# Moving filler work between two attention stages: memory gates earlier, forget sums later, two pairs of branch products begun early

## The chip, the cores and the metric

One core of a Trainium2 chip runs the whole program; the other cores are idle. The metric is device microseconds from the first to the last instruction of one execution, as a median over runs of the same program, lower is better.

## The reference

A decoder trunk of two layers on 512 tokens of width 1024. Each layer is a half-weighted SwiGLU block, a mixing block and a second half-weighted SwiGLU block, each between two RMS norms. The change lies in the mixing block, which is, cut to what matters:

```python
u = _rmsnorm(h, mix_pre_g[l])
q_sb, k_sb, v_sb, q_fx, k_fx, v_fx, f_logit, q_mem = jnp.split(u @ w_in[l], split_at, axis=-1)
o_sb = _stick_breaking_attention(q_sb, k_sb, v_sb)            # 8 heads of width 64
log_f = jax.nn.log_sigmoid(f_logit + b_forget[l])
o_fx = _forgetting_attention(q_fx, k_fx, v_fx, log_f)         # 8 heads of width 64
o_mem = _memory_attention(q_mem, k_mem, v_mem)                # 4 heads of width 128
g_sb, g_fx, g_mem = jnp.split(jax.nn.sigmoid(u @ w_gate[l] + b_gate[l]), 3, axis=-1)
merged = g_sb * (o_sb @ w_br_sb[l]) + g_fx * (o_fx @ w_br_fox[l]) + g_mem * (o_mem @ w_br_mem[l])
h = h + _rmsnorm(merged @ w_out[l], mix_post_g[l])
```

The stick-breaking weights come from a reversed running sum over the keys. The forgetting scores get a difference of running sums of `log_f`, ahead of a causal softmax. Both are row-wise work on 512 x 512 score tiles.

## The kernel before, in words

**Precision.** Every weight and activation is split into a rounded part and a remainder: ScalarE writes the rounded part (line 190 or 193), VectorE the remainder (line 191 or 194). A product is three matmuls into one PSUM bank (lines 216 to 218). Heavy products are 512 columns wide.

**Two streams on one TensorE.** In the mixing stage two streams of work are woven together by the program itself, before anything runs:

- The *chains* are the attention heads. A causal head has three steps on TensorE: the scores (`zs`, line 1305, for stick-breaking; `zf`, lines 1349 to 1357, for forgetting), ten 128 x 128 transposes of the probabilities (`pts` or `ptf`, line 1291, in `transposed`), and the product with the values (`pvs` or `pvf`, line 1278, in `attend`). Between the first two lies a row-wise chain on ScalarE and VectorE: for stick-breaking Abs, Exp, Ln (lines 1310 to 1312), an add (1313), a scan (1318), a subtraction (1321) and Exp (1322); for forgetting a maximum (1359), Exp (1361), a reciprocal (1362) and a scaling (1363). Heads come in pairs, first the four stick-breaking pairs, then the four forgetting pairs in the order 2, 3, 0, 1.
- The *queue* (`Q`) is a list of jobs that need no head at that moment: projections of the next pair (`pq`, `pk`), of values (`pv`), products of a finished branch with its output matrix (`pb`), memory gates (`pg`). A job is cut into single products; `weave` hands them out one at a time while a chain waits for its row-wise work. Each wait of a chain has a planned length in microseconds of TensorE work (12.0 and 4.7 for stick-breaking, 6.0 and 4.2 for forgetting), and a pair of heads has a *limit*, a place in the list that the queue may not pass while that pair runs. The limits of the stick-breaking pairs are cut at `marks["sb"]`, which stands just ahead of the first stick-breaking branch product, since that product needs all stick-breaking heads.

Where the list has no job left below the limit, the chain's next step follows directly, and TensorE stands still until the row-wise chain is done. The Tile framework then orders each engine's instructions by the order of the program and its own look at dependences, and each engine runs its list in that order.

**Jobs that the change moves.**

- `mem_gate(dp)` makes one pair of memory gates: 48 matmuls for two 128 x 512 tiles, two weight tiles to split, then Exp (204), a minimum (205), Ln (206), an add with maximum (211), Exp (212) and the product with the sum so far, `mg` (1651). There are four pairs; pairs 0 and 1 stand beside the first two stick-breaking pairs, pairs 2 and 3 beside the last two forgetting pairs.
- `forget_cumsum` makes the running sums `cs` of the forget logits: four transposes into `pfl` (1438), Abs, Exp, Ln on ScalarE, an add and a scan on VectorE (1445, 1446), and copies with their remainder to four places (1449 to 1452). Each forgetting head reads `cs` through `qk` (1340). It stands between the query and the key projection of the first forgetting pair.
- `merge(br, w, dp)` multiplies a branch by its output matrix (two tiles `pb`, each of four k-steps of three matmuls), fetches the saved gates `ga` from HBM by a DMA that GpSimd issues (1674), and adds gate times product to `mg` (1681, 1682). For the forgetting branch (`br` = 1) the four k-steps come in the order of the pairs 2, 3, 0, 1, so that the first three can be done before the last pair is finished. `early` = 3 cuts them off as a job of their own, `begin`, whose products (9 matmuls for each of two tiles) may be done while the last head runs; `run` does the fourth k-step and the rest. Before the change only the first of four pairs of tiles has this.

**Buffers.** PSUM has two rings of four banks: `mm` for products and `z` for scores and transposes. Row-wise tiles of the heads, the gates `ga` and the sums of `attend` share one ring of five SBUF tiles (`f32t`). Split weights have four buffers each, raw weights four.

Of the kernel before, what the change touches and what calls it, by code (L numbers as in the profile page):

```python
# [22 lines left out]
def kernel(  # L23
# [39 lines left out]
    _, S, D = x.shape  # L63
# [3 lines left out]
    ND = D // P  # L67
# [32 lines left out]
    def tmp(name):  # L100
        return sb.tile([P, S], F32, tag="f32t", bufs=5, name=name)
# [6 lines left out]
    def blk(tag, name):  # L108
        return stile([P, 2, S], tag, name)

    def pbank(tag, name):
        return ps.tile([P, S], F32, tag=tag, bufs=4, name=name)
# [95 lines left out]
    def sigmoid_neg(t, z, bias):  # L208

        log1p_exp(t, z, bias=bias)  # L210
        nc.vector.scalar_tensor_tensor(t, z, bias, t, ALU.add, ALU.max)
        nc.scalar.activation(t, t, AF.Exp, scale=-1.0)
# [7 lines left out]
    def gemm(pt, units, m, act, order=None, part=slice(None)):  # L220

        tiles = [(un, k) for un in units for k in range(un.nk)]
        order = order or range(len(tiles))
        for n in range(len(tiles))[part]:
            un, k = tiles[order[n]]
            c = slice(m * P, (m + 1) * P)
            ah, al = act(un.k0 + k)
            mm3(pt, un.h[:, k, c], un.l[:, k, c], ah, al, n == 0, n == len(tiles) - 1)
            yield 3 * pt.shape[1] * PE_US
# [5 lines left out]
    def list_act(ts):  # L235
        return lambda k, c=FULL: (ts[k][:, 0, c], ts[k][:, 1, c])
# [183 lines left out]
    def wpair(src, ktiles, c0, name, scale=None):  # L420

        return [Unit(src, k, min(4, ktiles - k), c0, 256, f"{name}_{k}", scale) for k in range(0, ktiles, 4)]
# [110 lines left out]
    Q = Queue()  # L533
# [895 lines left out]
    FOX = (2, 3, 0, 1)  # L1429

    def forget_cumsum(l, fl, holder):

        pt = pbank("mm", f"pfl{l}")
        for t in range(NT):
            nc.tensor.transpose(pt[:NH, t * P:(t + 1) * P], fl[:, t], ident[:])
        yield 0.3
        a, b = tmp(f"fa{l}")[:NH], tmp(f"fb{l}")[:NH]  # L1440

        nc.scalar.activation(a, pt[:NH], AF.Abs, bias=bfor[:, l:l + 1])
        nc.scalar.activation(a, a, AF.Exp, scale=-1.0)
        nc.scalar.activation(a, a, AF.Ln, bias=one_t[:NH])
        nc.vector.scalar_tensor_tensor(a, pt[:NH], nbfor[:, l:l + 1], a, ALU.min, ALU.subtract)
        nc.vector.tensor_tensor_scan(b, bfor[:, l:l + 1].broadcast_to([NH, S]), a, 0.0, ALU.add, ALU.add)
        cs = stile([P, S], "cs", f"cs{l}")
        nc.gpsimd.memset(cs[:].bitcast(F32), 0.0)
        nc.scalar.copy(cs[0:NH], b)
        nc.vector.tensor_tensor(cs[32:32 + NH], b, cs[0:NH].bitcast(F32), ALU.subtract)  # L1450
        for c in (0, 32):
            nc.gpsimd.tensor_copy(cs[64 + c:64 + c + NH], cs[c:c + NH])
        holder["cs"] = cs

    def mixing(l, src, ks, vs, values, dst):
# [5 lines left out]
        st, marks = {}, {}  # L1461
# [56 lines left out]
        def proj(key, un, scale):  # L1518
            nm = f"{key[0]}{l}_{key[1]}_{key[2]}"
            pt = pbank("mm", "p" + nm)  # L1520
            yield from gemm(pt[:], [un], 0, act)
            if key[0] == "q":

                t = st[key] = blk("q", nm)
                for r, ro, j in HEAD_ROWS:
                    split(t[r, j], t[ro, j], pt[r], scale=scale)
            else:

                twice = key[1] == 0
                t = st[key] = stile([P, 4 if twice else 3, S], "k", nm)  # L1530
                for r, ro, j in HEAD_ROWS:
                    split(t[r, j], t[r, 2 + j if twice else 2], pt[r])
                    if twice:
                        nc.gpsimd.tensor_copy(t[ro, j::2], t[r, j::2])
                    else:
                        nc.gpsimd.tensor_copy(t[ro, j], t[r, j])
# [15 lines left out]
        def project(br, p):  # L1552
            base = br * 1536
            marks["before", br, p] = len(Q.jobs)
            for x, off, scale in (("q", 0, 0.125), ("k", 512, None)):
                un1 = Unit(w_in[l], 0, ND, base + off + p * P, P, f"{x}{l}_{br}_{p}")
                marks[br, p] = Q.add([un1], lambda x=x, un1=un1, scale=scale: proj((x, br, p), un1, scale))
                if (br, p, x) == (1, FOX[0], "q"):
                    Q.add([], lambda: forget_cumsum(l, st["fl"], st))

        def factor(n):
# [78 lines left out]
        def mem_gate(dp):  # L1640
            ug = wpair(w_gate[l], ND, 2 * D + dp * 256, f"wg{l}_2_{dp}", scale=-1.0)

            def run():
                for m in range(2):
                    d = 2 * dp + m
                    pg = pbank("mm", f"pg{l}_2_{d}")
                    yield from gemm(pg[:], ug, m, act)
                    a = tmp(f"ga{l}_2_{d}")
                    sigmoid_neg(a[:], pg[:], nbgate[:, l, 2 * ND + d:2 * ND + d + 1])
                    md = st["merged"][dp][:, m]  # L1650
                    nc.vector.tensor_tensor(md, md, a[:], ALU.mult)
            Q.add(ug, run)

        def merge(br, w_br, dp, early=0):

            ub = wpair(w_br[l], NP, dp * 256, f"wb{l}_{br}_{dp}", scale=0.5)
            order = FOX if br == 1 else None
            gate, banks = [], []

            def products(m, part):  # L1660
                if len(banks) <= m:
                    banks.append(pbank("mm", f"pb{l}_{br}_{2 * dp + m}"))
                yield from gemm(banks[m][:], ub, m, list_act(st["o", br]), order, part)

            def begin():
                for m in range(2):
                    yield from products(m, slice(0, early))

            def run():
                for m in range(2):  # L1670
                    d = 2 * dp + m
                    gate.append(tmp(f"ga{l}_{br}_{d}"))
                    c = slice(d % 4 * S // 2, (d % 4 + 1) * S // 2)
                    nc.gpsimd.dma_start(gate[m][:].rearrange("p (i q) -> p i q", i=2),
                                        gsave[br, :, d // 4, :, c].rearrange("i p q -> p i q"))
                for m in range(2):
                    d = 2 * dp + m
                    a = gate[m]
                    yield from products(m, slice(early, NP))
                    md = st["merged"][d // 2][:, d % 2]  # L1680
                    nc.vector.scalar_tensor_tensor(a[:], a[:], 1.0, banks[m][:], ALU.add, ALU.mult)
                    nc.vector.tensor_tensor(md, md, a[:], ALU.add)
                    if br == 1:
                        mt = blk("v" if d < 4 else "qk"[d % 2], f"ms{l}_{d}")
                        split(mt[:, 0], mt[:, 1], md)
                        st["ms"].append(mt)

            if early:
                marks["begun", br] = Q.add(ub, begin)
                return Q.add([], run)  # L1690
            return Q.add(ub, run)

        marks["values"] = values
# [40 lines left out]

        heads = [(0, p) for p in range(NP)] + [(1, p) for p in FOX]
        project(*heads[0])
        project_v(*heads[0])
        marks["v"] = len(Q.jobs)
        for i, (br, _) in enumerate(heads):
            if i + 1 < len(heads):  # L1740
                project(*heads[i + 1])
            if br == 0:
                mem_branch(i)
                if i < 2:
                    mem_gate(i)
            else:
                if 4 < i < 7:
                    mem_gate(i - 3)
                if i == NP:
                    marks["sb"] = len(Q.jobs)  # L1750
                merge(0, w_br_sb, i - NP)
            if i in (2, 4):
                project_v(*heads[i + 2])
        marks["fox"] = len(Q.jobs)
        for dp in range(ND // 2):
            merge(1, w_br_fox, dp, 3 if dp == 0 else 0)


        limits = [marks["before", *h] for h in heads[2:]] + [marks["fox"], marks["begun", 1]]
# [183 lines left out]
    for l in LAYERS:  # L1943
        i, mn = 3 * l, []
# [42 lines left out]
```

## Time and profile before

| | |
|---|---|
| median of 3 runs | 2380.63 us (2379.75 to 2381.37) |
| the profiled execution, timed | 2379.89 us |
| span of the profiled execution | 2378.0 us |
| mean granted TensorE clock | 0.995 |
| causal heads, layer 0 | about 510 to 792 us of the span |
| causal heads, layer 1 | about 1689 to 1971 us of the span |

The two layers run the same program, so a stall in one is looked for in the other 1179 us later. In the profile PE is TensorE, DVE is VectorE, ACT is ScalarE, POOL is GpSimd. Rows of the timeline give the start, the duration, the engine, the line, the tiles written and read without buffer numbers, and in brackets the idle time of that engine just before with the instruction that ended it. A matmul's own duration (0.39 us at 512 columns) is longer than the distance between two of them, since they overlap; where work is counted, the distance of the starts is used.

### The profile page before, as it was taken

Reading aid. Unit: us, or ns where it says so; the run is one execution under the profiler, and the core shown is the slowest. Engines: PE = TensorE matmul, PEld = TensorE weight load, DVE = VectorE, ACT = ScalarE, POOL = GpSimd, SP = SyncE. Lnnn points to the kernel's source line nnn. Section 1 sums busy time; section 2 is a strip of 40 time slices with the busy share of each in tenths; the row PEclk is TensorE's granted clock in tenths of the full one; section 3 lists DMA queues with packets and bytes.
Section 4 is the critical chain, followed back from the end, with each engine's and each line's share of the span. In section 5 each row is a group of like instructions: output and inputs, shape, how many; then the busy total and the mean of one; then the engine's idle time right before and its main releaser. Section 6 shows DMA issues by size and latency. Waiting matters only on the chain.

```text
span 2378.0 us, 32025 instructions
## 1 busy us (share of the span) xinstructions
PE 2341.7 (98%) x11944; PEld 1991.1 (84%) x11944; DVE 1828.2 (77%) x2443; ACT 1484.0 (62%) x2406; POOL 255.3 (11%) x290
## 2 busy tenths in 40 slices
PE   9999999999989999999999999999998999999998
PEld 8888889988878788888888888899887888888887
DVE  8766978758877887769787679777688777866696
ACT  6656765667755465566665566657677554655574
POOL 1101001001112101101011110010011121110110
PEclk9999999999999999999999999999999999999999
DMA  8866858532312676759486767584322226876682
GB/s 248 235 173 182 226 190 234 167 109 63 89 54 80 219 217 168 193 151 263 161 220 170 188 191 224 188 242 138 107 72 81 63 89 213 222 186 177 181 226 98
DMA packets 237407, 398.03 MB, mean 167 GB/s; under 512 B 12458, under 2 KB 86466, under 8 KB 236740
## 3 DMA queue, kind: packets, MB, share of 16 engines
q1 hardware_dynamic: 197472, 312.06, 40.2%
q0 software_dynamic: 37472, 75.54, 17.3%
q10 hardware_dynamic: 2308, 8.39, 0.9%
q8 instruction: 94, 1.54, 0.3%
q14 instruction: 61, 0.50, 0.1%
HBM read 372.87 MB, written 23.07 MB: 167 GB/s over the span
## 4 chain that ended last, share of the span: by engine, by line
PE 88%; DVE 6%; issue 3%; DMA 2%; ACT 2%; DVEq 0%; SPq 0%; POOLq 0%; ACTq 0%
PE ptc L216 5%; PE ptc L218 5%; PE ptc L217 5%; PE pta L216 5%; PE pta L218 5%; PE pta L217 5%; PE pda L217 3%; PE pda L216 3%; PE pda L218 3%; PE pdc L218 3%; PE pdc L217 3%; PE pdc L216 3%; PE g L216 2%; PE g L218 2%; PE g L217 2%
## 5 line engine op out<-in xcount | busy, mean ns | idle before, releaser
L191 DVE TENSOR_TENSOR wl_tc<-ktc,wh_tc 128x1024 fp32r<-128x1024 f32 x80 | 97.7, 1223 | 63.3 <-ACT wh_tc L190 63.3
L191 DVE TENSOR_TENSOR wl_ta<-kta,wh_ta 128x1024 fp32r<-128x1024 f32 x80 | 97.6, 1223 | 57.7 <-ACT wh_ta L190 57.7
L190 ACT CAST wh_tc<-ktc 128x1024 fp32r<-128x1024 f32 x80 | 84.1, 1053 | 67.9 <-PE ptc L218 48.0
L218 PE MATMUL pta<-wh_ta,aga 128*128 128x512 f32 x320 | 124.7, 390 | 1.2 <-DVE aga L191 1.2
L216 PE MATMUL pta<-wh_ta,aga 128*128 128x512 f32 x320 | 125.4, 392 | 0.4 <-DVE sa L715 0.4
L216 PE MATMUL ptc<-wh_tc,agc 128*128 128x512 f32 x320 | 125.2, 393 | 0.0
L190 ACT CAST wh_ta<-kta 128x1024 fp32r<-128x1024 f32 x80 | 84.2, 1053 | 64.9 <-PE pta L218 41.8
L218 PE MATMUL ptc<-wh_tc,agc 128*128 128x512 f32 x320 | 124.6, 389 | 0.0
L217 PE MATMUL ptc<-wl_tc,agc 128*128 128x512 f32 x320 | 124.6, 389 | 0.0
L217 PE MATMUL pta<-wl_ta,aga 128*128 128x512 f32 x320 | 124.6, 389 | 0.0
L191 DVE TENSOR_TENSOR wl_ta<-raw_ta,wh_ta 128x1024 fp32r<-128x1024 f32 x58 | 70.9, 1223 | 44.6 <-ACT wh_ta L190 44.4
L191 DVE TENSOR_TENSOR wl_tc<-raw_tc,wh_tc 128x1024 fp32r<-128x1024 f32 x56 | 68.5, 1224 | 45.6 <-ACT wh_tc L190 45.6
L190 ACT CAST wh_ta<-raw_ta 128x1024 fp32r<-128x1024 f32 x58 | 60.9, 1052 | 48.3 <-PE pta L218 38.0
L190 ACT CAST wh_tc<-raw_tc 128x1024 fp32r<-128x1024 f32 x56 | 59.0, 1053 | 48.3 <-PE ptc L218 36.9
L216 PE MATMUL ptc<-wh_tc,us_b 128*128 128x512 f32 x224 | 87.7, 391 | 0.2
L216 PE MATMUL pda<-wh_da,aa 128*128 128x512 f32 x224 | 87.5, 391 | 0.0
L216 PE MATMUL pdc<-wh_dc,ac 128*128 128x512 f32 x224 | 87.5, 391 | 0.0
L218 PE MATMUL ptc<-wh_tc,us_b 128*128 128x512 f32 x224 | 87.2, 389 | 0.0
L218 PE MATMUL pda<-wh_da,aa 128*128 128x512 f32 x224 | 87.2, 389 | 0.0
L217 PE MATMUL ptc<-wl_tc,us_b 128*128 128x512 f32 x224 | 87.2, 389 | 0.0
L217 PE MATMUL pda<-wl_da,aa 128*128 128x512 f32 x224 | 87.2, 389 | 0.0
L217 PE MATMUL pdc<-wl_dc,ac 128*128 128x512 f32 x224 | 87.2, 389 | 0.0
(613 smaller groups left out, 7937.4 us busy)
## 6 DMA issues: line engine op xcount, KB each, us to landing
raw_ta<-in_ffn_w_gate_dram SPq DMA_DIRECT2D x44, 512.0 KB, 4.2
raw_wg<-in_w_gate_dram SPq DMA_DIRECT2D x44, 512.0 KB, 3.8
raw_tc<-in_ffn_w_gate_dram SPq DMA_DIRECT2D x44, 512.0 KB, 4.2
raw_da<-in_ffn_w_down_dram SPq DMA_DIRECT2D x42, 512.0 KB, 3.7
raw_dc<-in_ffn_w_down_dram SPq DMA_DIRECT2D x42, 512.0 KB, 3.3
kta<-in_ffn_w_up_dram SPq DMA_DIRECT2D x40, 512.0 KB, 6.1
ktc<-in_ffn_w_up_dram SPq DMA_DIRECT2D x40, 512.0 KB, 6.0
raw_wo<-in_w_out_dram SPq DMA_DIRECT2D x24, 512.0 KB, 3.4
```

The source lines that it names most:

```text
L190: both = [nc.scalar.copy(h_ap, src)]
L191: make = lambda: nc.vector.tensor_tensor(l_ap, src, h_ap.bitcast(F32), ALU.subtract)
L216: nc.tensor.matmul(pt, lh, rh, start=start, stop=False, skip_group_check=free)
L217: nc.tensor.matmul(pt, lh, rl, start=False, stop=False, skip_group_check=free)
L218: nc.tensor.matmul(pt, ll, rh, start=False, stop=stop, skip_group_check=free)
```

## The change

Three edits in the list of jobs, each for both layers.

- The memory gates of pairs 2 and 3 no longer stand beside the forgetting pairs 0 and 1. They stand behind the memory branch's last product at the fourth stick-breaking pair, ahead of the place `marks["sb"]`, and so below the limit of the last stick-breaking pair.
- `forget_cumsum` stands behind the key projection of the first forgetting pair, not ahead of it.
- The forgetting branch's second pair of products gets `early` = 3 too, and its two tiles are taken from the `z` ring. Both `begin` jobs are put ahead of both `run` jobs, and the limit of the last head stays at the first `begin`.

No instruction's work changes; what changes is the order on each engine, and with it which buffers follow each other in the rings.

```diff
-                if (br, p, x) == (1, FOX[0], "q"):
+                if (br, p, x) == (1, FOX[0], "k"):
                     Q.add([], lambda: forget_cumsum(l, st["fl"], st))
...
-        def merge(br, w_br, dp, early=0):
+        def merge(br, w_br, dp, early=0, tag="mm"):
...
-                    banks.append(pbank("mm", f"pb{l}_{br}_{2 * dp + m}"))
+                    banks.append(pbank(tag, f"pb{l}_{br}_{2 * dp + m}"))
...
             if early:
-                marks["begun", br] = Q.add(ub, begin)
-                return Q.add([], run)
+                marks["begun", br] = min(marks.get(("begun", br), 1 << 20), Q.add(ub, begin))
+                return lambda: Q.add([], run)
             return Q.add(ub, run)
...
             if br == 0:
                 mem_branch(i)
-                if i < 2:
-                    mem_gate(i)
+                for dp in ((0,), (1,), (), (2, 3))[i]:
+                    mem_gate(dp)
             else:
-                if 4 < i < 7:
-                    mem_gate(i - 3)
                 if i == NP:
                     marks["sb"] = len(Q.jobs)
                 merge(0, w_br_sb, i - NP)
...
-        for dp in range(ND // 2):
-            merge(1, w_br_fox, dp, 3 if dp == 0 else 0)
+        for rest in [merge(1, w_br_fox, dp, 3, tag) for dp, tag in enumerate(("mm", "z"))]:
+            rest()
+        for dp in range(2, ND // 2):
+            merge(1, w_br_fox, dp)
```

What stands on the engines now, at three places of layer 0. **TensorE ahead of the last stick-breaking head's transposes.** `pb` is the memory branch's last product, `pts_3_1` the transposes. Before:

```order
L216 MATMUL pb_2_7_6096<-om_3_4852,wh_wb_2_3_0_5753 128x512
L217 MATMUL pb_2_7_6096<-om_3_4852,wh_wb_2_3_0_5753 128x512
L218 MATMUL pb_2_7_6096<-om_3_4852,wl_wb_2_3_0_5754 128x512
L1291 MATMUL pts_3_1_0_6167<-ident,ts_3_1_1_6127 128x128 x2
L1291 MATMUL pts_3_1_0_6167<-ident,ts_3_1_2_6115 128x128
```

Now 42 matmuls of the memory gates `pg_2_4` and `pg_2_5` stand between that product and the transposes; the last of them are:

```order
L216 MATMUL pg_2_5_6203<-us_a_1_3057,wh_wg_2_2_4_5765 128x512
L217 MATMUL pg_2_5_6203<-us_a_1_3057,wh_wg_2_2_4_5765 128x512
L218 MATMUL pg_2_5_6203<-us_a_1_3057,wl_wg_2_2_4_5766 128x512
L1291 MATMUL pts_3_1_0_6224<-ident,ts_3_1_1_6121 128x128 x2
L1291 MATMUL pts_3_1_0_6224<-ident,ts_3_1_2_6109 128x128
```

The transposes follow gates instead of the memory branch; the remaining 54 gate matmuls stand behind them.

**TensorE ahead of the last forgetting head's transposes**, `ptf_1_1`; `pb_0_7` is a stick-breaking branch product, `zf` the scores. Before, the rows next to the transposes are (30 such branch matmuls stand between the head's scores and its transposes):

```order
L216 MATMUL pb_0_7_7457<-o_0_1_4152,wh_wb_0_3_0_7118 128x512
L217 MATMUL pb_0_7_7457<-o_0_1_4152,wh_wb_0_3_0_7118 128x512
L218 MATMUL pb_0_7_7457<-o_0_1_4152,wl_wb_0_3_0_7119 128x512
L1291 MATMUL ptf_1_1_0_7433<-ident,pf_1_1_0_7373 128x128
L1291 MATMUL ptf_1_1_0_7433<-ident,pf_1_1_1_7366 128x128
```

Now:

```order
L1356 MATMUL zf_1_1_2_7444<-k_1_1_7201,q_1_1_7114 128x384
L1357 MATMUL zf_1_1_2_7444<-qk_1_1_7328 128x384
L1278 MATMUL pvf_1_0_7478<-ptf_1_0_7401,v_1_0_0_6681 128x512
L1278 MATMUL pvf_1_0_7478<-ptf_1_0_7401,v_1_0_0_6681 128x384 x2
L1278 MATMUL pvf_1_0_7478<-ptf_1_0_7401,v_1_0_1_6757 128x256 x4
L1291 MATMUL ptf_1_1_0_7494<-ident,pf_1_1_0_7474 128x128
L1291 MATMUL ptf_1_1_0_7494<-ident,pf_1_1_1_7467 128x128
```

Only the previous head's seven value matmuls are left between the scores and the transposes; the branch products have moved ahead of them.

**GpSimd around the last forgetting pair's keys.** `ga_0_4` to `ga_0_7` are fetches of saved gates, `k_1_1` and `qk` are copies that the last pair's scores need. Before:

```order
L1536 COPY k_1_1_7149<-k_1_1_7149 64x512
L1338 COPY qk_1_0_7190<-k_1_1_7149 64x512
L1536 COPY k_1_1_7149<-k_1_1_7149 64x512
L1338 COPY qk_1_1_7232<-k_1_1_7149 64x512
L1261 MEMSET ptf_1_1_7431 128x128
L1674 DMA ga_0_4_7323<-gsave 128x2x256
L1674 DMA ga_0_5_7325<-gsave 128x2x256
```

Now:

```order
L1536 COPY k_1_1_7201<-k_1_1_7201 64x512
L1674 DMA ga_0_4_7214<-gsave 128x2x256
L1674 DMA ga_0_5_7216<-gsave 128x2x256
L1674 DMA ga_0_6_7278<-gsave 128x2x256
L1536 COPY k_1_1_7201<-k_1_1_7201 64x512
L1674 DMA ga_0_7_7280<-gsave 128x2x256
L1338 COPY qk_1_0_7286<-k_1_1_7201 64x512
L1338 COPY qk_1_1_7328<-k_1_1_7201 64x512
```

Four fetches stand between the key copies and ahead of the copies that feed the scores.

## The prediction

> **What bounds the kernel now.** First the page: busy times and the chain that ended last.
>
> ```profile
> span 2378.0 us, 32025 instructions
> PE 2341.7 (98%) x11944; PEld 1991.1 (84%) x11944; DVE 1828.2 (77%) x2443; ACT 1484.0 (62%) x2406; POOL 255.3 (11%) x290
> ```
>
> TensorE is busy for 2341.7 of 2378.0 us, so at most 36 us of waits can be won without touching its work. The change touches no work. Second view: for whom TensorE waited (total, times, longest).
>
> ```profile
> PE pts L1291 <- ACT ts L1322: 15.0, 2, 7.5
> PE pk L216 <- DVE ss L1282: 4.2, 2, 2.1
> PE pb L216 <- DVE ga L1681: 4.1, 2, 2.2
> PE zf L1349 <- DVE ptf L191: 1.2, 2, 0.6
> ```
>
> These four make 24.5 us, each once in either layer, all in the mixing stage. A wait also costs what comes behind it, so the third view is the windows around them: length, busy TensorE, weight loads, DVE, ACT, POOL, then the granted clock.
>
> ```profile
> 639.00:642.00 3.00, 0.90 (x6) 0.48 (x5) 2.94 (x6) 2.40 (x4) 0.34 (x1) 1.00 0.44 150
> 656.80:664.30 7.50, 0.02 (x1) 0.02 (x1) 7.43 (x12) 5.35 (x10) 0.00 (x0) 0.82 0.22 70
> 664.30:668.40 4.10, 4.10 (x18) 3.58 (x18) 1.83 (x5) 1.55 (x4) 0.00 (x0) 0.50 0.00 0
> 790.00:794.40 4.40, 2.16 (x13) 1.75 (x11) 1.64 (x2) 0.58 (x1) 0.33 (x1) 1.00 0.94 364
> 794.40:798.10 3.70, 3.70 (x10) 2.88 (x11) 2.58 (x4) 0.31 (x1) 1.26 (x2) 0.54 1.01 376
> 1843.00:1847.10 4.10, 4.10 (x21) 3.53 (x22) 2.11 (x5) 1.55 (x4) 0.00 (x0) 0.63 0.00 0
> 1972.10:1975.80 3.70, 3.64 (x9) 2.88 (x10) 2.59 (x5) 0.18 (x1) 1.14 (x2) 0.54 1.02 374
> ```
>
> Behind the 7.5 us wait TensorE runs 4.1 us at a clock of 0.50 (0.63 in layer 1): lost 4.1 x 0.50 = 2.05 and 4.1 x 0.37 = 1.52. Behind the 2.2 us wait it is 0.54 for 3.7 us, in both layers: lost 1.70 each. Around the 2.1 us wait at 640 the clock stays 1.00. **All that the change can take: 24.5 + 2.05 + 1.52 + 3.40 = 31.4 us.**
>
> **Part one: gates ahead of the last stick-breaking transposes.** These rows give the place, and the first and last of 30 products that run without a gap.
>
> ```profile
> 656.40 0.39 PE L218 MATMUL pb<-om,wl_wb 128*128 128x512 f32 x1
> 664.28 2.39 PE L1291 MATMUL pts<-ident,ts 128*128 128x128 f32 x10 [7.49 <-ACT ts L1322]
> 779.33 0.40 PE L216 MATMUL pb<-o,wh_wb 128*128 128x512 f32 x1
> 785.91 0.39 PE L218 MATMUL pb<-o,wl_wb 128*128 128x512 f32 x1
> ```
>
> A product takes (785.91 - 779.33) / 29 = 0.227 us of TensorE. The 42 gate products that now stand here are 9.5 us of cover for a 7.49 us wait. But TensorE also comes earlier, by the 2.1 us that part two removes: 656.63 - 2.1 + 9.5 = 664.0. When are the probabilities ready?
>
> ```profile
> 645.45 0.74 DVE L1445 SCALAR_TENSOR_TENSOR fa<-pfl,nbfor,fa 8x512 f32<-8x512 f32 x1 [0.28 <-ACT fa L1444]
> 646.94 1.21 DVE L1446 TENSOR_TENSOR_SCAN fb<-bfor,fa 8x512 f32<-8x512 f32 x1
> 649.78 0.98 DVE L1450 TENSOR_TENSOR cs<-fb,cs 8x512 fp32r<-8x512 f32 x1
> 653.10 1.70 DVE L1340 TENSOR_SCALAR qk<-cs,sel 40x512 fp32r<-40x512 f32 x2
> 655.66 0.69 DVE L1313 SCALAR_TENSOR_TENSOR ts<-zs,ts 128x512 f32<-128x512 f32 x1
> ```
>
> VectorE begins the head's chain at 655.66, and the transposes start 8.6 us later. In the new order the forget sums (0.74 + 1.21 + 0.98 + 1.70 = 4.6 us of VectorE) stand directly ahead of that chain, and their input comes later: the four `pfl` transposes now follow the key projection (24 x 0.227) and ten transposes, near 646.1, against 643.3 before. Upper end: the same 11.5 us from there to the end of the `qk` rows as before (643.3 to 654.8); the chain starts near 657.6, the transposes could start at 666.2, and TensorE waits 2.2. Lower end: nothing is held up, the scores come 1.6 us earlier than before, no wait. I take 1.3, nearer to the upper end, because VectorE runs its list in order and the sums are ahead in it. The weight split inside the chain is one as before (1.2 us), a gate's in place of a value projection's.
>
> Next, the first forgetting head's scores need the four `z` banks, which VectorE frees by splitting the transposes. A gate's steps stand ahead of these splits now.
>
> ```profile
> 650.79 1.69 DVE L191 TENSOR_TENSOR pts<-pts,pts 128x512 fp32r<-128x512 f32 x4
> 770.82 1.23 DVE L194 SCALAR_TENSOR_TENSOR wl_wb<-raw_wb,wh_wb 128x1024 fp32r<-128x1024 f32 x1 [0.74 <-ACT wh_wb L193]
> 771.96 0.42 DVE L205 TENSOR_SCALAR ga<-ga 128x512 f32<-128x512 f32 x1
> 773.17 0.75 DVE L211 SCALAR_TENSOR_TENSOR ga<-pg,nbgate,ga 128x512 f32<-128x512 f32 x1 [0.79 <-ACT ga L206]
> 776.12 0.69 DVE L1651 TENSOR_TENSOR mg<-mg,ga 128x512 f32<-128x512 f32 x1
> ```
>
> 0.42 + 0.75 + 0.69 + one weight split 1.23 + the splits 1.69 make 4.8, with about 0.6 of waiting for ScalarE between: 5.4 us from the transposes' start. TensorE's cover is ten transposes (1.0) and 15 gate products (3.4): a wait of 1.0, between 0 (if VectorE fits the gate in earlier) and 2.
>
> **Part two: forget sums behind the key projection.**
>
> ```profile
> 639.18 0.49 PE L1438 MATMUL pfl<-ident,fl 128*8 128x128 f32 x3
> 641.76 0.47 PE L216 MATMUL pk<-us_a,wh_k 128*128 128x512 f32 x1 [2.10 <-DVE ss L1282]
> ```
>
> The key projection waits 2.10 for the PSUM bank that a head's sum (`ss`) still reads. In the ring of four, `pfl` took the bank that had been free. Without it ahead, `pk` gets a value projection's bank, read out long before; the wait goes. What is late next is `pfl`'s user, counted above. Gone as well, by the new order there, is the 0.6 at `zf`: its keys now have 21 branch products (4.8 us) behind them.
>
> **Part three: the last head.** The gates that covered the forgetting pairs 0 and 1 are used up, and the branch products have moved up in their place. At the last head only seven value matmuls stay between scores and transposes.
>
> ```profile
> 764.92 0.28 PE L1357 MATMUL zf<-qk 104*128 104x256 f32 x1
> 767.44 0.55 DVE L1363 TENSOR_SCALAR pf<-pf,stf 128x256 f32<-128x256 f32 x2
> 777.87 0.57 PE L1357 MATMUL zf<-qk 128*128 128x512 f32 x2
> 778.27 1.21 PE L1278 MATMUL pvf<-ptf,v 128*128 128x512 f32 x7
> 785.39 0.28 DVE L1363 TENSOR_SCALAR pf<-pf,stf 128x128 f32<-128x128 f32 x1
> ```
>
> Head 1_0 had VectorE to itself: from its last score (765.20) to its last probability (767.99) 2.8 us. Head 1_1 shared it with gates and branch sums: 778.44 to 785.67, 7.2 us. In the new order no other work stands between the last head's maxima and its scalings, so the row to go by is the first: 2.8 and some 0.3 of hand-over, less a cover of 1.2, a wait of 1.9; by the second row it would be 6.0. One head earlier VectorE has a branch sum and a weight split ahead of the maxima and two more steps between them: I add a wait of 1.1 there (0 to 5), 0.5 for the `z` banks of the last scores, and 0.4 at the last value product, which follows its transposes at once: 3.9 together. In return the wait `pb <- ga` goes. It came from the gate fetches:
>
> ```profile
> 786.78 2.17 POOL L1674 DMA_DIRECT2D ga<-gsave  x3 [12.47 <-PE ptf L1291]
> 793.61 0.69 DVE L1681 SCALAR_TENSOR_TENSOR ga<-ga,pb 128x512 f32<-128x512 f32 x1 [2.65 <-DMA ga<-gsave]
> DMA to landing us min/median/max: 3.1/4.1/8.1
> ```
>
> The fetches waited for a tile that the last transposes free, and a bank waited for the fetch. Now these fetches are issued a head earlier, and behind the last transposes stand 21 products in three banks, two of them from the `z` ring, that need no gate: 4.8 us. Their last k-step needs the last head, some 2.8 us of splits after its value product, which the products of the second pair cover.
>
> **The clock.** A gap of 1.8 to 2.2 us cost 1.70 at the branch products and nothing at 640. For the 1.9 us wait I take half, 0.9 (0 to 1.7). [...]
>
> **The tail.** TensorE no longer waits ahead of the branch products, so VectorE's sums for the output projection have less lead: 0.4 allowed (0 to 1.5; no row shows it, the bound is one weight split, 1.23, and a little).
>
> **The sum.** Added per layer: 1.3 + 1.0 + 3.9 + 0.9 + 0.4 = 7.5, in two layers 15.0. Net: 31.4 - 15.0 = 16.4. The profiled execution took 2379.89; 2363.5 after the change. The median of the runs lies 0.74 above it: **2364 us**.
>
> **The rivals.**
>
> - *The gap only moves to the last head.* For it: the cover there falls from 30 products to none, and the 7.2 us row. Against it: nothing else is left on VectorE in that stretch. Then the wait is 6.0 instead of 1.9, and the clock falls as behind the 7.5 us wait (1.8 instead of 0.9): 5.0 more per layer, net 6.4, 2374. Chance 0.2.
> - *The waits fit in.* VectorE has room at both stick-breaking places and at head 1_0: only the 1.9 stays, 3.8 in all, net 27.6, 2353. Chance 0.15.
> - *The gates fill nothing.* If forget sums and gate steps push the stick-breaking chain itself by 9 us, the old wait returns with its clock (15.0 + 3.6) and two small waits (2 x 2.3) go: net 31.4 - 15.0 - 18.6 + 4.6 = 2.4, 2378. Against it: four forget rows of 4.6 us and no more stand there. Chance 0.05.
> - *Slower: GpSimd's list.* Four gate fetches now stand ahead of copies for the last pair's scores, and on VectorE a sum that needs a fetch stands ahead of head 1_0's maxima. Each microsecond of landing beyond the median 4.1 goes into the wait of head 1_0, and a long wait costs 1.8 of clock. At the longest landing seen, 8.1, that is 4.0 + 1.8, still a gain. It decides at 7.5 + 1.8 + x = 15.7, x = 6.4, a landing of 10.5 us; at 13 us: 2 x (7.5 + 1.8 + 8.9) - 31.4 = 5 slower, 2386. No fetch in that row takes that long. Chance 0.05.
>
> **How the numbers follow.** My forecast holds 0.55. Low ends everywhere give 2353, so the range starts at 2352; it ends at 2376, taking in the moved gap and leaving out the last two rivals. About 0.2%, 4.8 us, can be told from no change: faster than 2375.9 are the forecast, the room case and most of the moved gap, 0.87; within it the rest of that and the unfilled gates, 0.08; slower 0.05.
>
> **What would show it.** In the new profile: `pts <- ts` near 1.3 us per layer and `pk <- ss` gone; no half-clock spell near 662; `pb <- ga` gone; a wait `ptf` of about 2 us at the last head. I am wrong if `ptf` or `pts` waits 5 us or more, or if `zf` waits for GpSimd's copies.

## The result and the profile after

The changed kernel takes 2363.62 us (median of 4 runs, 2362.87 to 2364.89) against 2380.32 us for the kernel before (median of 4 runs): ratio 0.9930, interval 0.9913 to 0.9947, 16.7 us faster. The profiled execution took 2364.89 us, 15.0 less than that of the kernel before.

The page of the changed kernel, its busy times:

```profile
span 2362.8 us, 32037 instructions
PE 2339.0 (99%) x11944; PEld 1988.2 (84%) x11944; DVE 1827.1 (77%) x2443; ACT 1483.3 (63%) x2406; POOL 261.6 (11%) x290
```

For whom TensorE waits now in the mixing stage (total, times, longest):

```profile
PE ptf L1291 <- DVE pf L1363: 6.4, 4, 2.4
PE zs L1305 <- DVE pts L191: 2.4, 4, 0.9
PE pts L1291 <- ACT ts L1322: 2.1, 2, 1.0
PE zf L1349 <- DVE ptf L191: 1.4, 2, 0.7
PE pvs L1278 <- ACT mg L1637: 0.9, 2, 0.5
PE zf L1349 <- DVE pts L191: 0.3, 2, 0.2
```

`pk <- ss` and `pb <- ga` are gone, and `pts <- ts` has fallen from 15.0 to 2.1. `zs <- pts` is as before. The one large new entry is `ptf <- pf`: the transposes of the forgetting pair 1, the last two heads. Where the waits stand in layer 0, from TensorE's timeline (start, length, line, tiles, and in brackets the wait just before):

```profile
651.92 1.32 PE L1278 MATMUL pvs<-pts,v 128*128 128x512 f32 x6 [0.47 <-ACT mg L1637]
666.08 1.09 PE L1291 MATMUL pts<-ident,ts 128*128 128x128 f32 x8 [1.02 <-ACT ts L1322]
671.07 0.74 PE L1349 MATMUL zf<-causal,ident 128*128 128x128 bf16 x3 [0.17 <-DVE pts L191]
686.00 0.23 PE L1349 MATMUL zf<-causal,ident 128*128 128x128 bf16 x1 [0.67 <-DVE ptf L191]
776.17 1.28 PE L1291 MATMUL ptf<-ident,pf 128*128 128x128 f32 x10 [1.18 <-DVE pf L1363]
786.77 2.04 PE L1291 MATMUL ptf<-ident,pf 128*128 128x128 f32 x10 [2.39 <-DVE pf L1363]
```

VectorE ahead of the last stick-breaking chain, its splits behind the transposes of that chain, and GpSimd's copies that it waits for at 657.07:

```profile
654.90 0.73 DVE L1340 TENSOR_SCALAR qk<-cs,sel 64x512 fp32r<-64x512 f32 x1
657.07 0.49 DVE L1340 TENSOR_SCALAR qk<-cs,sel 40x512 fp32r<-40x512 f32 x1 [1.44 <-POOL cs L1452]
657.59 1.16 DVE L1313 SCALAR_TENSOR_TENSOR ts<-zs,ts 128x512 f32<-128x512 f32 x2
669.86 1.68 DVE L191 TENSOR_TENSOR pts<-pts,pts 128x512 fp32r<-128x512 f32 x4
```

```profile
654.22 1.13 POOL L1338 CAST qk<-k 64x512 fp32r<-64x512 f32 x1 [0.37 <-DVE k L191]
655.41 0.69 POOL L1452 CAST cs<-cs 8x512 fp32r<-8x512 f32 x1
656.43 0.61 POOL L1452 CAST cs<-cs 8x512 fp32r<-8x512 f32 x1
```

The chain starts at 657.59 and not at 655.66. GpSimd's list of the gate fetches around the last two heads:

```profile
762.57 2.17 POOL L1674 DMA_DIRECT2D ga<-gsave  x3
765.34 0.72 POOL L1674 DMA_DIRECT2D ga<-gsave  x1
788.16 2.90 POOL L1674 DMA_DIRECT2D ga<-gsave  x4 [18.29 <-PE ptf L1291]
```

The four fetches at 762.57 to 765.34 are those of the last four stick-breaking gates; two of them were issued at 786.78 before. No score waits for GpSimd, although these fetches now stand ahead of copies that the last pair's scores need.

### The profile page after: what moved, and what is told of

It is laid out like the page before. It is cut to its first block, busy times and chain, and to the rows that moved or that the text cites. A ratio compares the mean times of both kernels' runs of the same rounds, so it can differ in the third digit from the quotient of the medians.

```text
span 2362.8 us, 32037 instructions
## 1 busy us (share of the span) xinstructions
PE 2339.0 (99%) x11944; PEld 1988.2 (84%) x11944; DVE 1827.1 (77%) x2443; ACT 1483.3 (63%) x2406; POOL 261.6 (11%) x290
## 4 chain that ended last, share of the span: by engine, by line
PE 91%; DVE 4%; ACT 2%; DMA 1%; issue 1%; POOL 0%; DVEq 0%; SPq 0%; POOLq 0%; ACTq 0%
PE ptc L216 5%; PE ptc L218 5%; PE ptc L217 5%; PE pta L216 5%; PE pta L218 5%; PE pta L217 5%; PE pdc L218 3%; PE pdc L217 3%; PE pdc L216 3%; PE pda L218 3%; PE pda L217 3%; PE pda L216 3%; PE g L216 2%; PE g L218 2%; PE g L217 2%; PE pb L216 2%
```

## The experiments

Times are medians in microseconds. Each ratio is to the kernel before, measured beside it, with its 95% interval. The kernel before measured 2379.14 beside the first four kernels below, 2378.84 beside the repeated changed kernel and the three that follow it, 2380.77 beside the last one and 2379.39 beside the rest.

**One edit at a time.** The forget sums alone, in the kernel before:

```diff
-                if (br, p, x) == (1, FOX[0], "q"):
+                if (br, p, x) == (1, FOX[0], "k"):
```

> The kernel before with the forget sums alone moved behind the key projection. Theory (the sums delay the stick-breaking chain): the key projection's wait of 2.1 us goes, but TensorE then only arrives earlier at the last stick-breaking transposes, whose probabilities come later, since VectorE starts that chain near 657.6 (as in the changed kernel) and not at 655.7; the wait at the transposes grows from 7.5 to about 11 us, net 1.5 to 2 us slower per layer, 2380 + 3 = about 2383. Rival (the sums edit gives what the wait cost): 2.1 us gone per layer and the same 7.5 behind it, about 2376.

Measured 2380.99, ratio 1.0008 (0.9999 to 1.0017): 1.9 us slower by the medians, where the theory had 3; that is at the edge of what can be told, and certainly no gain of 4. TensorE's longest entry, and the row of the last stick-breaking transposes:

```profile
PE pts L1291 <- ACT ts L1322: 21.1, 2, 10.5
```

```profile
665.64 2.40 PE L1291 MATMUL pts<-ident,ts 128*128 128x128 f32 x10 [10.54 <-ACT ts L1322]
```

`pk <- ss` is gone, and the wait has gone to the transposes: 10.54 instead of 7.49. They start later (665.64 against 664.28), although TensorE comes earlier. The mechanism of the theory holds, the rival falls.

The gates alone, in the kernel before:

```diff
-                if i < 2:
-                    mem_gate(i)
+                for dp in ((0,), (1,), (), (2, 3))[i]:
+                    mem_gate(dp)
...
-                if 4 < i < 7:
-                    mem_gate(i - 3)
```

> The kernel before with the memory gates alone moved. Theory: the gates are cover for the 7.5 us wait and nothing else removes it: wait at the last stick-breaking transposes 0 to 0.5, the half-clock spell behind it gone (7.5 + 1.8 per layer), key projection's wait of 2.1 stays; at the last head a wait of about 2.4 us, and behind it the wait of a branch product for a fetched gate stays (about 2, with clock 1.7); added waits as in the changed kernel about 4 + 1.7 per layer. Net 9.3 - 5 = about 4 per layer, 2372. Rival (the sums edit is needed for the gates to fit): wait at the stick-breaking transposes above 3 us and the time not under 2376.

Measured 2367.34, ratio 0.9947 (0.9934 to 0.9959): 11.8 us faster, more than the 7 to 8 of the theory.

```profile
PE ptf L1291 <- DVE pf L1363: 6.9, 4, 2.4
PE pk L216 <- DVE ss L1282: 4.2, 2, 2.1
PE pb L216 <- DVE sf L1282: 1.4, 2, 0.7
```

```profile
762.89 2.16 POOL L1674 DMA_DIRECT2D ga<-gsave  x3
```

No row `pts <- ts` is left: the gates cover the 7.5 us without the sums' help. And there is no `pb <- ga`: this edit alone brings the gate fetches forward, to 762.89 as in the changed kernel, and removes the wait for the fetched gate, which the theory had left to the third edit. So this one edit gives the larger part of the whole change. What stands in its place is 0.7 per layer, at a product that needs the bank of the last value product.

The second pair begun early alone, in the kernel before, with the edits of `merge` shown above:

```diff
...
-        for dp in range(ND // 2):
-            merge(1, w_br_fox, dp, 3 if dp == 0 else 0)
+        for rest in [merge(1, w_br_fox, dp, 3, tag) for dp, tag in enumerate(("mm", "z"))]:
+            rest()
+        for dp in range(2, ND // 2):
+            merge(1, w_br_fox, dp)
```

> The kernel before with the second pair of branch products begun early alone. Theory: of all waits only the branch product's wait for a fetched gate (1.8 to 2.2) and the half-clock spell behind it (1.7) go, since 18 products that need no gate stand there; 2 x 3.7 = 7.4 us, about 2373, the fetches themselves are issued where they were. Rival (the fetches only come later into the way): the wait moves to the third pair, time 2378 to 2381.

Measured 2377.90, ratio 0.9993 (0.9984 to 1.0002): no change that can be told, and at the lower end of the rival's range. But the wait neither goes nor moves to the third pair:

```profile
PE pts L1291 <- ACT ts L1322: 15.0, 2, 7.5
PE pb L216 <- DVE ga L1681: 3.5, 2, 1.8
```

The wait for the gate stays where it was, at `pb_1_1`, which belongs to the first pair and comes before the new products in the list, and the fetches are issued as late as before. The theory falls.

Gates and sums, without the third edit:

> The changed kernel without the second pair begun early. Theory: the wait at the last head (2.4 us) stays, and the wait for a fetched gate comes back behind the last transposes, about 2 us and up to 1.7 of clock per layer: 2363.6 + 4 to 7.5 = about 2370. Rival (the gates moved earlier already freed the row tiles, so the fetches are in time): within 1 us of 2363.6.

Measured 2365.01, ratio 0.9938 (0.9925 to 0.9952); the changed kernel, measured again below, has 0.9936 (0.9924 to 0.9949). The theory's 4 to 7.5 us are not there; the rival, that the fetches are already in time, holds. In this place stands

```profile
792.70 0.50 PE L216 MATMUL pb<-o,wh_wb 128*128 128x512 f32 x1 [0.70 <-DVE sf L1282]
```

and 0.69 in layer 1. By the traces the third edit is worth these 1.4 us, not the gate's wait; the times agree with 1.4 and cannot show it.

The sums taken back out of the changed kernel:

> The changed kernel without the move of the forget sums. Theory (the sums edit trades waits): the key projection's wait of 2.1 comes back in each layer, with a half-clock spell of 1.7 in about half of the cases, and the waits of 1.0 and 0.5 around the last stick-breaking head and some 0.5 of the score waits go: about 1.1 us slower per layer, 2 us above the changed kernel, 2365.5. Rival (the sums edit is worth the whole 2.1 and its clock): 4.2 to 7.6 above, 2367.5 or more. Second rival (it is worth nothing): 2363.5.

Measured 2364.03, ratio 0.9936 (0.9924 to 0.9949), the changed kernel's own ratio. The waits moved as the theory says (`pk <- ss` 4.2 back, `pts <- ts` gone, the longest at `zf` from 0.7 to 0.2); `zs <- pts` also grew, from 2.4 to 3.7. The rival's 4.2 us or more are not seen, but the intervals reach 3 us to either side. Beside the gates alone (2367.34), gates and sums together (2365.01) had looked 2.3 us better. Between nothing and 2 us, the worth of the sums' move is not settled.

**The changed kernel again**, as the measure for the next three.

> The changed kernel as it is, to be compared with the next three on the same chip. Every theory: about 0.993 of the kernel before, the waits of its profile again (last head 2.4, last stick-breaking transposes 1.0 in each layer).

Measured 2363.32, ratio 0.9936 (0.9924 to 0.9949).

**Is one pair of gates enough?** Pair 3 goes behind the last stick-breaking branch product. There the gate multiplies a sum that already holds the stick-breaking part of its two tiles, so two of the eight output tiles are another function; the instructions are the same.

```diff
-                for dp in ((0,), (1,), (), (2, 3))[i]:
+                for dp in ((0,), (1,), (), (2,))[i]:
...
                 merge(0, w_br_sb, i - NP)
+                if i == 7:
+                    mem_gate(3)
```

> The changed kernel, but only gate pair 2 ahead of the last stick-breaking transposes; pair 3 stands behind the last stick-breaking branch product. Theory (what stands ahead of the transposes is 42 products, less than the 48 of one pair, and the other pair was the cover of the last head): the wait at the stick-breaking transposes stays at 1.0, the 2.4 at the last head falls to under 1 and its half-clock spell of 1.7 goes: about 3.5 us per layer, 7 us under the changed kernel. Rival (both pairs are needed ahead): transposes wait over 3 us, or the gates' row-wise steps hold the last head's chain, which waits 2 us or more again; time within 2 us of the changed kernel or above.

Measured 2362.41, ratio 0.9932 (0.9920 to 0.9945): 0.9 us under the changed kernel by the medians, where the theory had 7.

```profile
PE zf L1349 <- DVE pts L191: 4.2, 4, 1.8
PE pts L1291 <- ACT ts L1322: 2.0, 2, 1.0
PE ptf L1291 <- DVE pf L1363: 1.3, 2, 0.7
```

Both waits came out as the theory says, 1.0 and 0.7. It had overlooked nine products of pair 3 between the transposes and the first forgetting scores. Without them the scores wait for the `z` banks, 1.8 at the longest. Behind that wait a 128x256 score product took 0.42 us (670.79), against 0.28 for its like at full clock in the changed kernel (672.52): by this row the half clock moves there with the wait, an estimate that no window shows. The time is where the rival put it, for a reason that neither had.

**Does the idle time make the half clock?** Products that nobody reads fill the last head's wait, ten in layer 0 and four in layer 1:

```diff
+        last = name[0] == "f" and name[2:] == "_1_1"
+        pv = pbank("mm", "pv" + name) if last else None
+        for _ in range((10, 4)[int(name[1])] if last else 0):
+            nc.tensor.matmul(pv[:], q[:, j, :P], k[:, j, :S], start=True, stop=True, skip_group_check=True)
         tri = transposed(ptile, name)
...
-        attend(pbank("mm", "pv" + name), j, value, tri, ot, name)
+        attend(pv if last else pbank("mm", "pv" + name), j, value, tri, ot, name)
```

> The changed kernel with products that nobody reads in the last head's wait of 2.4 us: ten (2.3 us) in layer 0, four (0.9 us) in layer 1, written to the bank that the value product clears afterwards. Theory (the half clock follows from TensorE standing idle for more than about 1.8 us of one stretch of 3.41 us of a fixed grid): no half-clock spell in either layer, 1.7 us less in each, 3.4 us under the changed kernel, with about 1.5 us of idle left in layer 1. Rival (the clock falls for another reason, as the fetches of weights there at over 360 GB/s): the spells stay, no change in time.

Measured 2361.20, ratio 0.9926 (0.9914 to 0.9938): 2.1 us under the changed kernel, though work was added and none removed; all five runs (2361.01 to 2361.61) lie under all five of the changed kernel (2362.84 to 2364.73). The mean granted clock of the profiled execution is 0.999, and no half clock is seen at either place: in layer 0 the products behind the fill are 0.23 us apart (787.19 and 787.42), in layer 1 the window behind the wait has 1.00. The windows around the fill in layer 0, and around the 1.45 us wait that is left in layer 1 (length, TensorE busy, weight loads, DVE, ACT, POOL, granted clock, DMA share, GB/s):

```profile
783.00:786.40 3.40, 3.30 (x19) 2.58 (x19) 2.76 (x10) 2.63 (x10) 0.00 (x0) 1.00 0.86 340
1951.00:1954.40 3.40, 1.95 (x12) 1.46 (x11) 2.88 (x11) 2.73 (x9) 0.00 (x0) 1.00 0.92 372
1954.40:1957.80 3.40, 3.33 (x20) 2.71 (x20) 2.51 (x6) 1.90 (x5) 2.37 (x4) 1.00 0.23 72
```

The DMA traffic of 340 to 372 GB/s is nearly that of the changed kernel (344 GB/s in the window at 783.71, shown below), so the rival falls. The gain is below the 3.4 of the theory; the section on the clock says why.

**Do GpSimd's copies hold the chain?** One of the two goes to ScalarE:

```diff
-        for c in (0, 32):
-            nc.gpsimd.tensor_copy(cs[64 + c:64 + c + NH], cs[c:c + NH])
+        nc.scalar.copy(cs[64:64 + NH], b)
+        nc.gpsimd.tensor_copy(cs[96:96 + NH], cs[32:32 + NH])
```

> The changed kernel with one of the two copies of the forget sums taken from GpSimd to ScalarE. Theory (VectorE's 1.4 us wait for these copies holds the last stick-breaking chain, which is why the transposes wait 1.0): VectorE starts the chain about 1 us earlier, the wait at the transposes falls to about 0 to 0.3, 0.7 to 1 us less per layer, about 1.5 to 2 us under the changed kernel. Rival (ScalarE's or VectorE's total work there sets the end): the wait stays at 1.0 or grows, no change.

Measured 2359.83, ratio 0.9919 (0.9906 to 0.9933): 3.5 us under the changed kernel. VectorE, then TensorE:

```profile
655.74 0.49 DVE L1340 TENSOR_SCALAR qk<-cs,sel 40x512 fp32r<-40x512 f32 x1 [0.85 <-POOL cs L1452]
656.26 1.15 DVE L1313 SCALAR_TENSOR_TENSOR ts<-zs,ts 128x512 f32<-128x512 f32 x2
```

```profile
664.66 0.33 PE L1291 MATMUL pts<-ident,ts 128*128 128x128 f32 x1 [0.34 <-ACT ts L1322]
```

The chain starts 1.3 us earlier and the wait is 0.34 instead of 1.02, as the theory says. That is 1.4 us for two layers. The span of the profiled execution fell by 4.1 us: beside the 1.4, 0.7 lie ahead of the causal heads, where the edit changes nothing (the first score starts at 510.00 and not at 510.71). What the other 2.0 are, and how the 3.5 us of the medians divide, is not shown.

**Do the two add?** The copy on ScalarE with ten unread products in both layers:

> The changed kernel with the copy on ScalarE and ten unread products in the last head's wait in both layers. Theory (the two effects lie in different places and add): 2359.8 less the 2.1 that the unread products gave, about 2357.7, no half-clock spell in the layers, the wait at the last head gone from the list since the products stand in it. Rival (the sum is smaller, since the earlier arrival only waits elsewhere): 2359 or more.

Measured 2358.89, ratio 0.9914 (0.9900 to 0.9927). Against the copy alone (0.9919) that is 0.0005 x 2379 = 1.2 us less, where the theory had 2.1. The mean granted clock of the profiled execution is 0.999, against 0.998 with the copy alone; no window shows whether a half-clock spell is left. The intervals do not tell 1.2 from 2.1, or from the rival's smaller sum.

**Real cover for the last head, first try.** With the copy on ScalarE, pair 3 stands ahead of the last stick-breaking branch products, and the queue may go on to the next projections behind the stick-breaking transposes:

```diff
-                for dp in ((0,), (1,), (), (2, 3))[i]:
+                for dp in ((0,), (1,), (), (2,))[i]:
...
+                if i == 7:
+                    mem_gate(3)
...
+        limits[NP - 1] = marks["sb"]
```

> The changed kernel with the copy on ScalarE, gate pair 3 directly ahead of the last stick-breaking branch products instead of ahead of the transposes, and the queries and keys of the second forgetting pair allowed as cover behind the last stick-breaking transposes. Theory (branch products that move towards the end fetch their gates only after the last transposes): no wait over 0.5 at the last head and none over 1 at the first forgetting scores, but a wait of about 2 us for a gate fetch comes back where the last value product needs the bank of the sixth branch product; about 1 us better per layer than with the copy alone, 2357 to 2358. Rival (the fetch is hidden): no such wait, 2354 or less. Second rival (the gates' row-wise steps hold the last head): a wait of 2 us or more at its transposes, 2360 or more.

Measured 2363.70, ratio 0.9927 (0.9914 to 0.9941). The two waits at the last head's value product in layer 0, and two windows from the start of the half clock on:

```profile
784.86 1.79 PE L1278 MATMUL pvf<-ptf,v 128*128 128x512 f32 x5 [2.32 <-DVE ga L1681]
787.44 1.01 PE L1278 MATMUL pvf<-ptf,v 128*128 128x256 f32 x3 [0.80 <-DVE ptf L191]
```

```profile
785.15:788.56 3.41, 2.61 (x9) 2.10 (x8) 3.38 (x7) 0.07 (x1) 1.45 (x2) 0.50 0.74 271
788.56:791.98 3.42, 3.42 (x9) 2.65 (x9) 1.73 (x3) 1.12 (x2) 1.13 (x2) 0.50 0.74 227
```

The wait for a late gate fetch came back at the named place, 2.32. The price was wrong: a second wait stands behind it, and the half clock lasts two windows, 6.8 us; the mean granted clock of this execution is 0.996. By the ratios the kernel is 1.9 us slower than with the copy alone, where 2 us faster was expected; the runs spread from 2358.11 to 2365.17. The second rival named such a time, but its wait at the transposes is not there.

**Second try.** The copy on ScalarE, and each forgetting head keeps a little less planned cover, so that nine branch products are left for the last one:

```diff
-    W_FX0, W_FX1 = 6.0, 4.2
+    W_FX0, W_FX1 = 5.7, 4.2
```

> The changed kernel with the copy on ScalarE and the planned wait of the forgetting transposes cut from 6.0 to 5.7, which hands nine real branch products (2.0 us) on to the last head's wait. Theory (the cover is enough in sum and lies in the wrong place): wait at the last head 2.4 less 2.0, about 0.4, no half-clock spell in the layers (worth 2.1 in all with the unread products), 0.3 to 0.7 more at the head before it; about 2.0 + 1.1 - 0.5 = 2.6 per layer under the 2359.8 of the copy alone, 2355. Rival (the fetches of the last two stick-breaking gates now stand behind head 1_0's transposes, and their row tiles hold up the last head's probabilities): the wait at the last head stays at 2 us or more, 2359 or above.

Measured 2354.74, ratio 0.9895 (0.9878 to 0.9911), the fastest of all: 26 us under the kernel before, and by the ratios 5.7 us under the copy alone, though the two intervals just overlap.

```profile
PE ptf L1291 <- DVE pf L1363: 3.2, 2, 1.6
PE zf L1349 <- DVE ptf L191: 1.4, 4, 0.8
```

The time is as expected, the split is not: the last head still waits 1.6, not 0.4, since the two steps of a branch sum (between 777.77 and 779.51) now stand ahead of and among its maxima on VectorE. But the waits of head 1_0 went (1.2 and 0.5 in the changed kernel), and all four runs have a mean granted clock of 0.999; whether the 1.6 us of idle cost clock, no window shows.

## The clock: why the same wait costs 1.7 us or nothing

In the traces of the kernel before and of the changed kernel the granted clock of the layers is 1.00 or 0.50. A half-clock spell there lasts 3.41 us (from 787.13 in the changed kernel) or 6.83, twice that (from 661.59 in the kernel before), and in one execution all begin on one grid: in the kernel before at 661.59, 794.71, 1839.18 and 1972.30, in the changed kernel at 787.13 and 1957.90. With a step of (1972.30 - 661.59) / 384 = 3.413 us these are 39, 345 and 384 steps from the first, and 343 steps apart. So windows were laid on that grid, first in the kernel before, around `pk <- ss` (639.67 to 641.76) and `pb <- ga`:

```profile
637.69:641.11 3.42, 1.98 (x11) 1.28 (x9) 3.39 (x8) 2.27 (x5) 0.00 (x0) 1.00 0.58 153
641.11:644.52 3.41, 2.76 (x13) 2.21 (x14) 3.33 (x7) 2.81 (x6) 1.06 (x2) 1.00 0.00 0
...
791.29:794.71 3.42, 1.18 (x8) 0.93 (x8) 0.69 (x1) 0.58 (x1) 0.00 (x0) 1.00 0.98 380
794.71:798.12 3.41, 3.41 (x10) 2.63 (x9) 2.58 (x4) 0.33 (x1) 1.28 (x2) 0.50 1.00 374
```

Then around the last head's 2.4 us wait in the changed kernel, and around the same wait without the sums' move:

```profile
783.71:787.13 3.42, 1.03 (x9) 0.86 (x8) 2.90 (x11) 2.73 (x9) 0.00 (x0) 1.00 0.84 344
787.13:790.55 3.42, 3.42 (x14) 3.03 (x13) 2.37 (x6) 1.90 (x5) 2.39 (x4) 0.50 0.23 78
```

```profile
781.54:784.95 3.41, 2.38 (x15) 1.87 (x13) 2.21 (x8) 1.67 (x6) 0.00 (x0) 1.00 0.94 375
784.95:788.36 3.41, 1.98 (x13) 1.69 (x14) 2.45 (x8) 2.40 (x8) 0.91 (x2) 1.00 0.39 157
788.36:791.78 3.42, 3.42 (x19) 2.94 (x18) 2.10 (x5) 1.14 (x4) 1.98 (x3) 1.00 0.71 224
```

A window in which TensorE was idle 2.24 or 2.39 us is followed by one at 0.50. A wait that the grid splits, 1.44 and 0.65, or 1.03 and 1.43, is followed by full clock. In the layers of the two traces, full-clock windows with 1.44 us of idle or less were followed by full clock and those with 2.04 (1954.49 in the changed kernel) or more by half; 1.82 stood in the kernel before once ahead of full clock (1818.70) and once ahead of half (1968.89). With the second pair alone 1.74 was followed by full clock (789.73), without the sums' move 1.90 by half (1808.89). From these rows the border is taken as 1.8, and for a wait of 2.4 us that gives an estimate of the chance: its first part lies 1.8 or more in one window for starts in the first 1.61 of 3.41 us, its second part for the last 0.58, together 0.64, if every place on the grid is as likely and no other idle lies in the window. In the changed kernel both such waits (2.39 and 2.38) were followed by half clock, without the sums' move the one in layer 0 was not. Times 1.7 us, the estimate is 1.1 per wait and 2.2 for two, against the 2.1 that the unread products gave. The grid and the border are readings of these traces; the fill showed the cause, idle time.

## Why the prediction was right, step by step

Forecast and profile per layer, in microseconds of time added; the waits are from the rows above and their like in layer 1:

| step | forecast | layer 0 | layer 1 |
|---|---|---|---|
| last stick-breaking transposes | 1.3 | 1.02 | 1.04 |
| first forgetting head, scores | 1.0 | 0.17 | 0.17 |
| second forgetting head, scores | none | 0.67 | 0.68 |
| value product, for a bank that ScalarE copies to `mg` | none | 0.47 | 0.47 |
| head 1_0, transposes | 1.1 | 1.18 | 0.47 |
| last head, scores | 0.5 | 0 | 0 |
| last head, transposes | 1.9 | 2.39 | 2.38 |
| last value product | 0.4 | 0 | 0 |
| half clock | 0.9 | 1.7 | 1.7 |
| tail | 0.4 | 0 | 0 |
| sum | 7.5 | 7.6 | 6.9 |

31.4 less 14.5 is 16.9; the two profiled executions differ by 15.0, and the medians by 16.7. The 1.9 us between the profiled executions and the sum is in no row of this stage; some 0.5 of it are small waits at the stage boundaries.

- *Gates ahead of the transposes.* Right, and shown by the gates alone. The forecast start of VectorE's chain, 657.6, is the row 657.59; the forecast upper end of the transposes' start, 666.2, is 666.08. That agreement is partly luck: the stretch from the `pfl` transposes to the `qk` rows was carried over as 11.5 us and measured 10.9, but its contents changed. ScalarE took up the sums at once before, and now only at 649.31, 2.6 us after the transposes; VectorE needs 6.1 us from `fa` to the last `qk` row and not 9.4. The wait was still only 1.0, because TensorE came at 666.08 - 1.02 = 665.06 and not at 664.0. The cause was half right: of the sums, it is GpSimd's copies that VectorE waits for, 1.44 us, which the forecast did not name.
- *The first forgetting scores.* Mis-sized. VectorE's part came as forecast: its splits end at 671.54, 5.5 us after the transposes started. But the scores took the four banks one after another, the first at 670.66 while the splits still ran, so 0.17 us of the 1.0 was left. The 0.67 at 686.00 is another wait, at the pair's second head behind the first head's transposes, which the forecast did not have.
- *The forget sums.* `pk <- ss` went, as said. The removal was booked as a gain of 2.1 per layer, and its price under another step; alone the edit gives no gain.
- *The gate fetches.* "These fetches are issued a head earlier" is right. That 21 products without a gate were needed behind it was wrong: the third edit alone leaves the wait, the first without the third removes it, because it is the first that brings the fetches forward.
- *The last head.* The row of head 1_0 was the right one to go by. From the end of the last score to the end of the last probability,

```profile
783.00 0.34 PE L1357 MATMUL zf<-qk 128*128 128x384 f32 x1
```

```profile
786.34 0.29 DVE L1363 TENSOR_SCALAR pf<-pf,stf 128x128 f32<-128x128 f32 x1
```

  it took 786.63 - 783.34 = 3.3 us, not 2.8, with 1.2 of cover as counted. The rival of 6.0 did not come (with the hand-over of 0.3 that the forecast counts in its 1.9, it would have been 6.3).
- *The clock.* "Half" of 1.7 is near the estimate for the mean over executions (1.1), and was too little for the profiled one, which paid in full twice (0.50 for 3.41 us from 787.13 and from 1957.90).
- *The terms for the last scores, the last value product and the tail*, 1.3 together, did not come (no such row is in the list of waits).

So the total fits more closely than its terms, and that is luck: in layer 0 some 2.4 us of terms that came smaller or not at all met 2.5 us that were larger or not foreseen (0.8 of clock, 0.7 at the second forgetting head, 0.5 at `mg`, 0.5 at the last head).

## What to carry to other kernels

Cover has a place as well as a size: 42 gate products closed a 7.5 us wait, and with no such cover left at the end one of 2.4 opened. Handing nine products on to the last head, by a planned wait of 5.7 instead of 6.0 us at every forgetting head, made it 1.6, and the mean granted clock of the runs was 0.999. An edit that takes a wait away ahead of a slower chain only moves the wait, so look at what is late next before booking the gain; the forget sums are the example. And in this kernel the price of a wait of 2.4 us depended on where it fell on the grid, 1.7 of clock or nothing, while full-clock windows with 1.44 us of idle or less in the two traces, and one with 1.74, were followed by full clock; so count the clock of a longer wait with a chance.

## What the runs showed of the hardware

- In the traces of the two kernels the granted clock of the layers went to 0.50 only on a grid of 3.413 us, which lay differently in the two executions (794.71 and 787.13 are 2.2 steps apart). It went there behind windows with 1.82 us of idle (1968.89 in the kernel before) to 3.41 (658.18 there), and stayed at 1.00 behind another with 1.82 (1818.70) and behind all full-clock ones with 1.44 or less. With 0.80 us of idle inside the half-clock window it stayed at half for another (785.15 in the first try for the last head), with 2.69 too (661.59 in the kernel before); with 0.40 (1842.60 there) and with none (787.13 in the changed kernel) it went back to full.
- Fourteen added products that nobody reads, ten of them (2.4 us of TensorE) in place of a wait in layer 0 and four in layer 1, made the kernel 2.1 us faster.
